# 80 tokens' experts gathered instead of 64, with the one-hots and the gates' copies dealt out anew

## The chip, the core and the metric

The kernel runs on one core of a Trainium2 chip. Its engines work side by side: TensorE (PE; its weight loads are the row PEld), VectorE (DVE), ScalarE (ACT), GpSimd (POOL) and SyncE (SP), the last of which here only issues transfers. They meet by semaphores. Matrix products go into PSUM banks, everything else lies in SBUF (128 partitions). The metric is the device time of one execution, in microseconds.

## The reference

One layer of an encoder step for 288 tokens (256 of a prompt, 32 new ones), each a row of 2048 numbers in fp32: differential attention, attention into 256 memory rows, an output projection, a norm, then a mixer of experts, and a second norm. The change is about the mixer. It has 128 x 128 experts, each one row of `u_tab` and one of `v_tab`. A token picks 16 of them in each of 8 heads, so 128 in all, by the sums of two scores (first key, second key):

```python
q = (xt @ w_q).reshape(T, 8, 2, 128)
s = jnp.einsum('thcd,hcnd->thcn', q, sub_keys)
sv, si = lax.top_k(s, 16)
cand = (sv[:, :, 0, :, None] + sv[:, :, 1, None, :]).reshape(T, 8, 256)
cidx = (si[:, :, 0, :, None] * 128 + si[:, :, 1, None, :]).reshape(T, 8, 256)
best, pos = lax.top_k(cand, 16)
experts = jnp.take_along_axis(cidx, pos, axis=-1).reshape(T, 128)
gates = jax.nn.softmax(best, axis=-1).reshape(T, 128)
...
    act = jnp.einsum('td,tkd->tk', xs, u_tab[es])
    h = jax.nn.gelu(act, approximate=False) * gs
    return jnp.einsum('tk,tkd->td', h, v_tab[es])
```

The result is `layer_norm(ALPHA * x1 + peer_ffn(x1))` with `x1` the rows behind the first norm.

## The kernel before

**Two ways for the mixer.** For 224 tokens (`ND`, the dense ones) every expert is computed, and the gates, mostly zero, pick. For the last 64 tokens the rows of their own experts are gathered from DRAM.

**The stream.** Everything large (projection weights, 256 units of `u_tab`, 256 of `v_tab`; a unit is 128 x 1024 numbers, 512 KB) is in a list `plan`, in the order of its use. `stream` (L131) keeps it running ahead of TensorE: SyncE loads a unit into one of four `raw` tiles, ScalarE casts it to the upper part `hi` (L165), VectorE makes `lo = raw - hi` (L181), both in three tiles in turn, up to two units ahead. So each product of fp32 numbers is made as two or three products of parts.

**Activations of the dense tokens** (from L1025). `x1` of the dense tokens lies in `ux` as [hi | lo], 2 x 224 columns. A block of 128 experts has two units of 8 pairs: L1039 multiplies `hi` weights with all 448 columns, L1041 `lo` weights with 224. `finish_act` adds the two halves of the bank (ScalarE's copy L992, an identity product L994) and applies GELU into `bigA` (the first 96 blocks, `SPLIT`) or `bigB`.

**Gates of the dense tokens.** From block 64 (`G0`) on, each unit also advances `gate_jobs`. For two tokens `one_hots` makes the one-hots of the second key on VectorE (L970) and those of the first key, with the gate as their height, on ScalarE (four instructions, L974 and L975); L1019 multiplies them, so that a bank gets the 128 x 128 gates of four tokens. `gate_in` brings these to the blocks: where the activation is already there VectorE multiplies it (L985), where it isn't VectorE copies the gates aside (L987), and `finish_act` multiplies later (L1004). With two tokens a unit this takes 112 units.

**The gathered tokens.** Their choices are made first: `topk` works on two heads at once, four heads of 64 tokens on each half of the partitions, so that a partition stands for a token and one of two groups of heads. `Rows` then fetches half rows of 1024 numbers by indirect DMA on GpSimd's queue (L948) into a ring of three tiles: when VectorE has used a half row, the third after it is issued. There are 64 steps of two half rows, 128 for `u_tab` (`use_u`, L963, a product with `x1g` and its sum) and 128 for `v_tab` (`use_v`, L1111, a multiple of the row added to `vacc`). They are spread evenly over the units: the first 40 (`GFIRST`) ahead of block 64, the rest up to the end of the activations; those of the values up to unit 230 (`VEND`).

**Values** (from L1199). Two halves of the columns, 128 units each; L1200 multiplies `hi` values with [hi | lo] of the gated activations (448 columns), L1202 `lo` values with 224, into eight banks that stay for a half. The last two or three units of a half form a group in which one bank after the other ends: `evac` copies (L1117), adds by a product (L1119) and sums into `yT` (VectorE, L1120); in the second half `turn` (L1190) transposes `yT` into banks that are free, and VectorE takes statistics (L1193) for the second norm of the dense tokens behind it.

**Work beside the stream.** A `tick`, two to a unit in the activations and one to a unit in the values, lets each generator in `stages` take a step, and the first one in `slow` spend its `pace`, by the cost that each step yields. So `topk`, `rows_job` (the rows `x1g`) and, behind the last gathered value, `finish_gathered` are paid out. `finish_gathered` folds the upper half of the partitions onto the lower (a transfer, then L1146), normalises the 64 rows (statistics L1151; ScalarE L1159; L1161 and L1163) and stores them (L1164). What of `slow` is left when the last group of values begins is issued at once, between that group's splits and its products.

## Time and profile before

| | us |
|---|---|
| median of three runs | 2014.75 |
| lowest, highest | 2012.73, 2016.01 |
| span of the profiled execution, first to last instruction | 2008.1 |
| median less span (the profiled execution is not timed apart) | 6.7 |
| activations with gates, 960 to 1290 us: PE, DVE, ACT busy, of 330.0 | 330.0, 302.7, 310.3 |
| values, 1360 to 1900 us: PE, DVE, ACT busy, of 540.0 | 539.7, 455.9, 271.4 |
| transfers in these two stretches | 297 and 327 GB/s |

The busy time of an engine in a stretch says how near it is to setting the pace there; the share over the whole span mixes stages. TensorE overlaps its instructions, so that their durations add to more than the time: the distance from one start to the next is what one costs.

### The profile page before, as it was taken

The numbers are of one execution on the slowest core, as the hardware profiler recorded it, in microseconds if no ns is written. First come the engines' busy times: TensorE is split into PE (matmuls) and PEld (weight loads), VectorE is DVE, ScalarE is ACT, GpSimd is POOL, SyncE is SP. The second block draws the span as 40 slices with busy tenths as digits, with TensorE's granted clock in tenths as the row PEclk, the third lists the DMA queues.
The fourth block names the chain that finished last, engine by engine and source line by source line (L and its number), as shares of the span: only waits on it lengthen the run. The fifth ranks groups of instructions, "written<-read, shape, count | busy, mean of one in ns | idle before, by whom it ended". The sixth has DMA issues, their size and how long they took to land.

```text
span 2008.1 us, 34989 instructions
## 1 busy us (share of the span) xinstructions
PE 1983.6 (99%) x13178; PEld 1872.5 (93%) x13178; DVE 1567.3 (78%) x2683; ACT 1160.7 (58%) x1919; POOL 480.9 (24%) x348
## 2 busy tenths in 40 slices
PE   9999999999999999999999999999999999999996
PEld 7999999999999999999999999999999999999996
DVE  5455555556788889998899999978888888888886
ACT  5345545544534555555999999854455555444553
POOL 0110000010000112222333333324443343334412
PEclk9999999999999999999999999999999999999998
DMA  8854555484445788888888888889999998999985
GB/s 294 258 165 141 153 155 153 129 287 137 154 148 162 241 291 280 277 282 283 294 298 296 293 298 302 300 288 318 335 322 343 327 333 314 323 328 321 327 264 167
DMA packets 147625, 521.21 MB, mean 260 GB/s; under 512 B 16848, under 2 KB 21088, under 8 KB 147328
## 3 DMA queue, kind: packets, MB, share of 16 engines
q1 hardware_dynamic: 103504, 360.49, 54.8%
q0 software_dynamic: 43952, 158.48, 22.0%
q8 instruction: 104, 1.70, 0.3%
q14 instruction: 65, 0.53, 0.1%
HBM read 508.33 MB, written 10.06 MB: 258 GB/s over the span
## 4 chain that ended last, share of the span: by engine, by line
PE 96%; DMA 1%; DVE 1%; ACT 1%; POOL 0%; issue 0%; SPq 0%; POOLq 0%; ACTq 0%; DVEq 0%
PE pa L1039 22%; PE pa L1200 11%; PE pb L1200 11%; PE pa L1041 11%; PE pa L232 8%; PE pa L233 7%; PE pa L234 7%; PE pb L1202 5%; PE pa L1202 5%; PE pb L1019 3%; DMA raw<-in_wmk 1%; PE pa L994 1%; PE pb L397 0%; DVE lo L181 0%; PE pa L893 0%; PE pa L319 0%
## 5 line engine op out<-in xcount | busy, mean ns | idle before, releaser
L181 DVE TENSOR_TENSOR lo<-raw,hi 128x1024 fp32r<-128x1024 f32 (+1 forms) x679 | 820.8, 1211 | 367.1 <-ACT hi L165 356.7
L165 ACT CAST hi<-raw 128x1024 fp32r<-128x1024 f32 (+1 forms) x679 | 705.5, 1040 | 497.2 <-PE pa L1200 253.8
L1039 PE MATMUL pa<-ux,hi 128*128 128x448 f32 x2048 | 669.8, 379 | 0.0
L1041 PE MATMUL pa<-ux,lo 128*128 128x224 f32 x2048 | 543.6, 265 | 0.0
L1039 PEld LDWEIGHTS pa<-ux,hi 128*128 128x128 f32 x2048 | 385.4, 188 | 29.4 <-issue 0.2
L1041 PEld LDWEIGHTS pa<-ux,lo 128*128 128x128 f32 x2048 | 391.7, 191 | 0.0
L948 POOL DMA_INDIRECT ur<-in_u,gidx x128 | 197.9, 1546 | 700.2 <-DVE ur L963 329.8
L1200 PE MATMUL pa<-hs,hi 128*128 128x448 f32 x1020 | 338.3, 376 | 0.0
L1200 PE MATMUL pb<-hs,hi 128*128 128x448 f32 x1020 | 338.0, 376 | 0.0
L948 POOL DMA_INDIRECT vr<-in_v,gidx x128 | 221.4, 1730 | 354.7 <-DVE x1g L1111 321.2
L1202 PE MATMUL pb<-hs,lo 128*128 128x224 f32 x1020 | 271.1, 266 | 0.3 <-DVE lo L181 0.3
L1202 PE MATMUL pa<-hs,lo 128*128 128x224 f32 x1020 | 271.0, 266 | 0.0
L1200 PEld LDWEIGHTS pb<-hs,hi 128*128 128x128 f32 x1020 | 191.4, 188 | 17.5
L1200 PEld LDWEIGHTS pa<-hs,hi 128*128 128x128 f32 x1020 | 191.4, 188 | 17.4
L1202 PEld LDWEIGHTS pb<-hs,lo 128*128 128x128 f32 x1020 | 195.1, 191 | 0.5 <-DVE lo L181 0.5
L232 PE MATMUL pa<-xh,hi 128*128 128x288 f32 x640 | 195.2, 305 | 0.0
L1202 PEld LDWEIGHTS pa<-hs,lo 128*128 128x128 f32 x1020 | 195.1, 191 | 0.0
L233 PE MATMUL pa<-xl,hi 128*128 128x288 f32 x640 | 188.9, 295 | 0.0
L234 PE MATMUL pa<-xh,lo 128*128 128x288 f32 x640 | 188.2, 294 | 0.0
L1111 DVE SCALAR_TENSOR_TENSOR x1g<-vr,ggate,x1g 128x1024 f32<-128x1024 f32 x128 | 163.7, 1279 | 0.0
L963 DVE SCALAR_TENSOR_TENSOR ur<-ur,x1g 128x1024 f32<-128x1024 f32 x128 | 155.7, 1216 | 0.0
L232 PEld LDWEIGHTS pa<-xh,hi 128*128 128x128 f32 x640 | 120.0, 188 | 4.9 <-issue 3.7
(346 smaller groups left out, 2706.7 us busy)
## 6 DMA issues: line engine op xcount, KB each, us to landing
raw<-in_ut SPq DMA_DIRECT2D x256, 512.0 KB, 4.4
raw<-in_v SPq DMA_DIRECT2D x255, 512.0 KB, 6.5
raw<-in_win SPq DMA_DIRECT2D x80, 512.0 KB, 3.7
raw<-in_wq SPq DMA_DIRECT2D x32, 512.0 KB, 3.6
raw<-in_wo SPq DMA_DIRECT2D x29, 512.0 KB, 3.7
raw<-in_wmv SPq DMA_DIRECT2D x8, 512.0 KB, 5.3
raw<-in_wmk SPq DMA_DIRECT2D x6, 512.0 KB, 5.8
xn<-in_xn POOLq DMA_DIRECT2D x8, 384.0 KB, 9.7
```

The costliest lines, as they stand in the source:

```text
L165: nc.scalar.copy(hi[:, cs], raw[:, cs])
L181: nc.vector.tensor_sub(lo, raw, hi.bitcast(F32))
L232: nc.tensor.matmul(ps[:, :n], wh, mh[:, d, :n], start=(d == 0), stop=False)
L233: nc.tensor.matmul(ps[:, :n], wh, ml[:, d, :n], start=False, stop=False)
L234: nc.tensor.matmul(ps[:, :n], wl, mh[:, d, :n], start=False, stop=(d == DT - 1))
L948: nc.gpsimd.indirect_dma_start(out=t, out_offset=None, in_=self.table, in_offset=bass.IndirectOffsetOnAxis(ap=gidx[:, a, s:s + 1], axis=0))
L963: nc.vector.scalar_tensor_tensor(rows, rows, 1.0, x1g[:, a * 1024:(a + 1) * 1024], op0=OP.mult, op1=OP.mult, accum_out=gact[:, a, s:s + 1])
L1039: nc.tensor.matmul(ps[:, :2 * ND], wh, ux[:, d].rearrange("p a t -> p (a t)"), start=(d == 0), stop=False, skip_group_check=True)
L1041: nc.tensor.matmul(ps[:, :ND], wl, ux[:, d, 0], start=False, stop=False, skip_group_check=True)
L1111: nc.vector.scalar_tensor_tensor(va, rows, ggate[:, s:s + 1], va, op0=OP.mult, op1=OP.add)
L1200: nc.tensor.matmul(accs[dt][:, :2 * ND], wh, hb.rearrange("p a t -> p (a t)"), start=(i == 0), stop=False, skip_group_check=True)
L1202: nc.tensor.matmul(accs[dt][:, :ND], wl, hb[:, 0], start=False, stop=False, skip_group_check=True)
```

## The change

16 tokens more, numbers 208 to 223, have their experts gathered. They get 32 steps' halves of their own: their 8 heads lie on 8 groups of 16 partitions in a second tile `x1b`, which is filled by eight small transfers, and steps from 64 on use it. So `ND` is 208, the dense products have 416 and 208 columns, the gates take 104 units, and there are 160 half rows for each table. `gathered_choice` waits for a ninth selection of the gathered tokens (`topk([(2, 4, 20)])`, one head for 128 partitions). `topk` does two heads in one instruction where it can. The one-hots of the second key are made for four tokens at once; `gate_in`'s copies go to ScalarE. `finish_gathered` folds `vacc` once and `x1b` three times (64, 32, 16 rows), moves 16 rows behind the 64, and has the norm on 80. `SPLIT` becomes 88 and the buffers of `xr` five. Cut to its core:

```diff
-ND = 224
+ND = 208
+NA = 224
+SLOTS = 80
+STEPS = 2 * SLOTS
-SPLIT = 96
+SPLIT = 88
-GFIRST = 40
+GFIRST = 48
...
+        for h in range(8):
+            nc.gpsimd.dma_start(x1b[16 * h:16 * h + 16], xn[80:96, 1])
+        for x, own_rows in ((x1g, xn[:, 2]), (x1b, x1b)):
...
+            nc.gpsimd.dma_start(s_all[16 * h:16 * h + 16, 20], s_all[80:96, 8 + h])
...
-                        slow.insert(at1 + 1, gathered_choice())
+                        slow.insert(at1 + 1, topk([(2, 4, 20)]))
+                        slow.insert(at1 + 2, gathered_choice())
...
     def use_u(s, a, rows):
+        x = x1g if s < 64 else x1b
...
+    def second_hots(t0):
+        Bt = big[2].tile([P, 4, NKEY], F32, tag="ohB", name=f"ohB{t0}")
+        nc.vector.tensor_tensor(out=Bt, in0=iota.unsqueeze(1).to_broadcast([P, 4, NKEY]),
+                                in1=e2T[:, t0:t0 + 4].unsqueeze(2).to_broadcast([P, 4, NKEY]), op=OP.is_equal)
+        return Bt
...
             if a < n:
-                nc.vector.tensor_copy(bt[:, a:n, t0:t0 + 4], pg[:, i0 + a:i0 + n])
+                nc.scalar.copy(bt[:, a:n, t0:t0 + 4], pg[:, i0 + a:i0 + n])
...
-                    ug.upto(GFIRST + (128 - GFIRST) * (n + 1 - 2 * G0) // (2 * (NKEY - G0) - 4))
+                    ug.upto(GFIRST + (STEPS - GFIRST) * (n + 1 - 2 * G0) // (2 * (NKEY - G0) - 4))
...
-        up = [gat.tile([P, 1024], F32, tag="rows", name=f"up{c}") for c in range(2)]
-        for c in range(2):
-            nc.gpsimd.dma_start(up[c][:64], vacc[64:128, c * 1024:(c + 1) * 1024])
-        yield 4.0
...
+        for x, w in ((vacc, 64), (x1b, 64), (x1b, 32), (x1b, 16)):
+            up = [gat.tile([P, 1024], F32, tag="rows", name=f"up{num()}") for c in range(2)]
+            for c in range(2):
+                nc.gpsimd.dma_start(up[c][:w], x[w:2 * w, c * 1024:(c + 1) * 1024])
+            yield 4.0
+            for c in range(2):
+                cs = slice(c * 1024, (c + 1) * 1024)
+                nc.vector.tensor_add(x[0:w, cs], x[0:w, cs], up[c][:w])
+                yield 1.15
+        nc.gpsimd.dma_start(vacc[64:SLOTS], x1b[0:16])
         yield 4.0
...
-                vg.upto(128 * (n + 1 - v_from) // (VEND - v_from))
-                if vg.used == 128:
+                vg.upto(STEPS * (n + 1 - v_from) // (VEND - v_from))
+                if vg.used == STEPS:
                     slow.append(finish_gathered())
```

The first place is VectorE among the units with gates. Before, two units and a bit of them (lines as above: splits L181, one-hots L970, gates L985 and L987, a gathered half row L963, the late product L1004):

```order
L181 TENSOR_TENSOR lo_12842<-raw_12767,hi_12841 128x1024
L970 TENSOR_TENSOR ohB_12864<-iota,e2T 128x256
L985 TENSOR_TENSOR bigA<-bigA,pb_12794 128x92x4
L987 COPY bigA<-pb_12794 128x4x4
L987 COPY bigB<-pb_12794 128x32x4
L963 SCALAR_TENSOR_TENSOR ur_0_12721,gact<-ur_0_12721,x1g 128x1024
L181 TENSOR_TENSOR lo_12884<-raw_12806,hi_12883 128x1024
L970 TENSOR_TENSOR ohB_12909<-iota,e2T 128x256
```

VectorE after the change, at a like place; the lines are 1 to 13 numbers later there (L184 are the splits, L964 the half rows, L990 the gates, L1009 the late product):

```order
L184 TENSOR_TENSOR lo_11570<-raw_11494,hi_11569 128x1024
L970 TENSOR_TENSOR ohB_11595<-iota,e2T 128x512
L964 SCALAR_TENSOR_TENSOR ur_1_11486,gact<-ur_1_11486,x1g 128x1024
L1009 TENSOR_TENSOR bigA<-bigA,tmp_11592 128x52
L184 TENSOR_TENSOR lo_11608<-raw_11532,hi_11607 128x1024
L990 TENSOR_TENSOR bigA<-bigA,pb_11557 128x78x4
L964 SCALAR_TENSOR_TENSOR ur_0_11527,gact<-ur_0_11527,x1g 128x1024
L184 TENSOR_TENSOR lo_11648<-raw_11572,hi_11647 128x1024
```

The copies L987 are gone from VectorE, a one-hot instruction stands in every second unit, and half rows stand in more of the units.

ScalarE in the same stage, before (casts L165, one-hots L974 and L975, `finish_act` L992, L1000 and L1002):

```order
L974 ACTIVATE ohA_13803<-iota,e1T 128x128
L975 ACTIVATE ohA_13803<-ohA_13803,gT,ngT 128x128
L992 CAST small_13818<-pa_13740 128x224
L165 CAST hi_13821<-raw_13744 128x1024
L1000 ACTIVATE tmp_13844<-pa_13740 128x160
L1002 ACTIVATE bigB<-pa_13740 128x64
```

ScalarE after (casts L168, one-hots L979 and L980, the gates' copies L992, `finish_act` L997, L1005 and L1007):

```order
L979 ACTIVATE ohA_11552<-iota,e1T 128x128
L980 ACTIVATE ohA_11552<-ohA_11552,gT,ngT 128x128
L992 COPY bigA<-pb_11479 128x11x4
L992 COPY bigB<-pb_11479 128x40x4
L997 CAST small_11566<-pa_11490 128x208
L168 CAST hi_11569<-raw_11494 128x1024
L1005 ACTIVATE tmp_11592<-pa_11490 128x52
L1007 ACTIVATE bigA<-pa_11490 128x156
```

The two copies of a bank's gates now stand on ScalarE ahead of the small copy and the next cast.

The second place is VectorE at the end of the values, in the last group (L1120 are the sums into `yT`, L1193 the statistics of transposed rows). Before:

```order
L181 TENSOR_TENSOR lo_21682<-raw_21629,hi_21681 128x1024
L181 TENSOR_TENSOR lo_21702<-raw_21653,hi_21701 128x256 x4
L1120 SCALAR_TENSOR_TENSOR yT<-yT,pb_18636 128x224
L1120 SCALAR_TENSOR_TENSOR yT<-yT,pb_18639 128x224
L1120 SCALAR_TENSOR_TENSOR yT<-yT,pb_18644 128x224
L1193 BN_STATS nst_15445<-pb_21753 128x6
```

VectorE there after (L1159 is a fold's addition, L1167 to L1143 the statistics and what follows from them, L1177 and L1179 the norm's rows, L1133 the sums into `yT`):

```order
L184 TENSOR_TENSOR lo_21532<-raw_21488,hi_21531 128x256 x4
L1159 TENSOR_TENSOR x1b<-x1b,up_21412 16x1024
L1167 BN_STATS nst_21545<-x1g 80x6 x4
L1141 BN_AGGR nmr_21546<-nst_21545 80x2
...
L1143 SCALAR_TENSOR_TENSOR nmr_21546<-nmr_21546 80x1
L1177 TENSOR_TENSOR x1g<-x1g,gb_21543 80x1024
L1179 TENSOR_TENSOR x1g<-x1g,gb_21544 80x1024
L1177 TENSOR_TENSOR x1g<-x1g,gb_21568 80x1024
L1179 TENSOR_TENSOR x1g<-x1g,gb_21569 80x1024
L1133 SCALAR_TENSOR_TENSOR yT<-yT,pb_18445 128x208
L1133 SCALAR_TENSOR_TENSOR yT<-yT,pb_18448 128x208
```

The last fold and the whole norm of the gathered tokens, which before stand among earlier units, now stand between the last split and the first sum into `yT`.

GpSimd's queue at the same place after (L1161 moves the 16 rows, L1146 are norm rows, L1180 and L1181 stores):

```order
L1161 DMA x1g<-x1b 16x2048
L1146 DMA gb_21543<-in_lnrow 80x1024
L1146 DMA gb_21544<-in_lnrow 80x1024
L1180 DMA out_y<-x1g 64x1024
L1181 DMA out_y<-x1g 16x1024
L1146 DMA gb_21568<-in_lnrow 80x1024
L1146 DMA gb_21569<-in_lnrow 80x1024
```

Here the second pair of norm rows stands behind the stores of the first half; it goes into tiles of the ring of three.

## Rows read from the trace of the kernel before

**Rows 1.** The page, parts 1 and 2: engines, and GB/s in 40 slices.
```profile
PE 1983.6 (99%) x13178; PEld 1872.5 (93%) x13178; DVE 1567.3 (78%) x2683; ACT 1160.7 (58%) x1919; POOL 480.9 (24%) x348
...
GB/s 294 258 165 141 153 155 153 129 287 137 154 148 162 241 291 280 277 282 283 294 298 296 293 298 302 300 288 318 335 322 343 327 333 314 323 328 321 327 264 167
```

**Rows 2.** Groups by line: count, then busy us, mean ns, and idle time before.
```profile
L1039 PE MATMUL pa<-ux,hi 128*128 128x448 f32 x2048 | 669.8, 379 | 0.0
L1200 PE MATMUL pa<-hs,hi 128*128 128x448 f32 x1020 | 338.3, 376 | 0.0
```

**Rows 3.** Timeline of TensorE in the activations: start and duration in us.
```profile
702.89 0.38 PE L1039 MATMUL pa<-ux,hi 128*128 128x448 f32 x1
703.11 0.27 PE L1041 MATMUL pa<-ux,lo 128*128 128x224 f32 x1
703.22 0.27 PE L994 MATMUL pa<-small,identr 128*128 128x224 f32 x1
703.32 0.38 PE L1039 MATMUL pa<-ux,hi 128*128 128x448 f32 x1
```

**Rows 4.** Timeline of TensorE's weight loads at the same place.
```profile
703.11 0.19 PEld L994 LDWEIGHTS pa<-small,identr 128*128 128x128 f32 x1
703.22 0.19 PEld L1039 LDWEIGHTS pa<-ux,hi 128*128 128x128 f32 x1
```

**Rows 5.** Timeline of TensorE in the memory's and the first projections.
```profile
60.30 0.40 PE L319 MATMUL pa<-lo,memh 128*128 128x512 f32 x1
60.53 0.40 PE L320 MATMUL pa<-hi,meml 128*128 128x512 f32 x1
...
90.12 0.29 PE L234 MATMUL pa<-xh,lo 128*128 128x288 f32 x1
90.25 0.30 PE L232 MATMUL pa<-xh,hi 128*128 128x288 f32 x1
```

**Rows 6.** Stretches: us; busy PE, PEld, DVE, ACT, POOL; clock; DMA share; GB/s.
```profile
420.00:422.00 2.00, 2.00 (x17) 2.00 (x16) 1.93 (x9) 0.65 (x1) 0.58 (x1) 1.00 1.02 397
960.00:1290.00 330.00, 330.00 (x2235) 315.67 (x2234) 302.65 (x587) 310.25 (x708) 121.42 (x77) 1.00 0.85 297
1360.00:1900.00 540.00, 539.73 (x3409) 509.89 (x3409) 455.90 (x395) 271.40 (x275) 217.44 (x129) 1.00 0.93 327
```

**Rows 7.** ScalarE's groups by line and shape, 960 to 1290 us; L616: whole run.
```profile
L165 ACT CAST hi<-raw 128x1024 fp32r<-128x1024 f32 x109 | 113.8, 1044 | 0.0
...
L616 ACT COPY ot<-pa 128x128 f32<-128x128 f32 x16 | 4.3, 272 | 0.0
```

**Rows 8.** Groups by line and shape, VectorE, 1360 to 1900 us.
```profile
L181 DVE TENSOR_TENSOR lo<-raw,hi 128x1024 fp32r<-128x1024 f32 x213 | 260.7, 1225 | 82.3 <-ACT hi L165 75.4
L1111 DVE SCALAR_TENSOR_TENSOR x1g<-vr,ggate,x1g 128x1024 f32<-128x1024 f32 x121 | 154.8, 1279 | 0.0
```

**Rows 9.** Gathers: issues 1350 to 1930 us (median to landing); line 948, both tables.
```profile
vr<-in_v,gidx POOLq DMA_INDIRECT x125, 8.2
...
DMA to landing us min/median/max: 4.0/7.3/11.1
```

**Rows 10.** The end: timelines of VectorE and TensorE; VectorE's groups 1925 to 1975; issues.
```profile
1981.87 0.39 DVE L1120 SCALAR_TENSOR_TENSOR yT<-yT,pb 128x224 f32<-128x224 f32 x1 [0.88 <-PE pb L1119]
...
1983.79 0.60 PE L1190 MATMUL pb<-ident,yT 128*128 128x128 f32 x4
...
L1151 DVE BATCH_NORM_STATS2 nst<-x1g 64x6 f32<-64x512 f32 x4 | 2.6, 675 | 0.0
L1161 DVE TENSOR_TENSOR x1g<-x1g,gb 64x1024 f32<-64x1024 f32 x2 | 2.4, 1208 | 0.0
L261 DVE RECIPROCAL rs<-rs 64x1 f32<-64x1 f32 x1 | 0.2, 156 | 1.4 <-ACT rs L259 1.4
...
out_y<-x1g POOLq DMA_DIRECT2D x2, 256.0 KB, 4.4
```

**Rows 11.** Timeline of VectorE in the query projection; in brackets the idle time before.
```profile
535.89 1.23 DVE L181 TENSOR_TENSOR lo<-raw,hi 128x1024 fp32r<-128x1024 f32 x1 [3.40 <-ACT hi L165]
```

More of the change, by code (lines that the diff above doesn't have):

```diff
@@ L679, in topk @@
[L679 to L685 removed]
+        n, t, R = len(units), units[0][0], ROWS[units[0][0]]
+        key = f"{t}_{units[0][1]}"
+        step = units[-1][1] - units[0][1] or 1
+        hs = slice(units[0][1], units[-1][1] + 1, step)
@@ new lines, in new @@
+        def new(tag, shape, dt=F32):
+            return tw.tile([P, 2] + shape, dt, tag=tag, name=f"{tag}{key}")[:R, :n]
+        S = [s_all[:R, u] for *_, u in units]
+        sv, si, sf = new("sv", [2, K]), new("si", [2, K], U32), new("sf", [2, K])
+        s2, ca, pos = new("s2", [2, NKEY]), new("ca", [K, K]), new("pos", [K], U32)
+        ab, abf = new("ab", [2, K], U32), new("abf", [2, K])
+        bv = best[:R, t, hs]
+        both = [(q, c) for c in range(2) for q in range(n)]
+        for q, c in both:
+            V.max(out=sv[:, q, c, 0:8], in_=S[q][:, c])
@@ L742, in gates @@
+        yield 0.62 * n
+        for c, en in ((0, e1n), (1, e2n)):
+            V.tensor_reduce(out=en[:R, t, hs], in_=eq[c], op=OP.add, axis=AX.X)
+        yield 0.62 * n
     def gates(t, nh):
@@ L1006, in gate_jobs @@
     def gate_jobs():
-        hots, banks = {}, {}
+        first, second, banks = {}, {}, {}
         n2 = ND // 2
@@ L1073, in tile_stream_step @@
         stages.append(g)
-    assert ug.used == 128 and gated == ND
+    assert ug.used == STEPS and gated == ND
     ohs.close()
```

202 lines of the change are left out of this document (89 added, 113 removed).

## The prediction

> **What bounds the kernel now.** I read the page first: TensorE is busy in 99% of the span, and no other engine comes near that [rows 1]. Then the groups of instructions by line and shape: the two expert stages hold 2048 pairs of products in the activations (lines 1039 and 1041) and 2 x 1020 in the values (lines 1200 and 1202, in two kinds of banks), 4088 in all [rows 2]. Then TensorE's timeline, since the durations of the groups overlap and only the distance between two starts says what an instruction costs: the product with 448 columns holds the engine 0.22 us, the one with 224 columns 0.10 to 0.11 [rows 3]. In neither stage does TensorE stand idle, so the span is the sum of these distances. The other engines are read by stage: while the gates are made (960 to 1290 us) ScalarE is busy 310 of 330 us and VectorE 303; in the values (1360 to 1900 us) VectorE is busy 456 of 540 us and the transfers run at 327 GB/s with the DMA engines 93% busy [rows 6]. So TensorE is the bound, with three followers close behind it.
>
> **What a pair loses.** The change takes 16 tokens out of the dense products: 448 columns become 416, 224 become 208. Beyond that the count of products stays. Longer products give the slope: 512 columns are 0.23 us apart, 288 columns 0.13 [rows 5], so (0.23 - 0.13) / 224 = 0.45 ns a column, and the long product loses 32 x 0.45 = 14.3 ns. The short one is another matter. Weights of 128 columns are loaded before each product, and two loads follow each other 0.11 us apart at the closest [rows 4]; where two short products stand in a row (line 994 behind line 1041) they too take 0.11 and 0.10 us [rows 3]. The load has the same size whatever the number of tokens, so I take the short product to be at the load's pace already and to lose nothing. Ends: 0 for the pair if both halves are held by loads, 14.3 + 16 x 0.45 = 21.5 ns if none is. I take 14.3, since [rows 3] and [rows 4] show the same 0.11. Sum: 4088 x 14.3 ns = 58.5 us. The Trainium skill ("TensorE: Matmul & The Clock Gate", Back-to-back issue gap) gives an isolated product N/2.4 + 2.5 ns; by that, an estimate, a pair would go from 285 to 265 ns and the change would bring 82 us. The trace has 0.32 us a pair, so the rule misses what the loads cost, and the sum goes by the rows.
>
> Fewer tokens also have gates. A unit (half an expert, 8 pairs) takes 330 / 109 = 3.03 us with gates [rows 6, 7] and 8 x 0.317 + 0.05 = 2.58 without; 208 tokens need 104 such units, not 112, so 8 x 0.45 = 3.5 us go. **TensorE's part: 62 us.** A unit then wants 8 x 14.3 = 115 ns less: 2.92 us with gates, 2.42 in the values.
>
> **What the followers give back, stage by stage.** With gates: ScalarE is busy 310.25 / 109 = 2.85 us a unit now [rows 6, 7]. It gets 75 copies that VectorE made before (87 there), 104 columns on average; a copy of 128 columns from PSUM takes it 0.27 us [rows 7]. That is 75 x 0.27 / 104 = 0.19 us a unit at most, and some 0.11 if neighbours overlap by 0.1 us. ScalarE would want 2.95 to 3.03 us where TensorE wants 2.92. VectorE stays where it is: 2.78 us a unit now, plus (112 - 88)/124 = 0.19 more half rows (by the code's spread over 124 units) at 1.3 us = +0.24, less 0.07 for four one-hots in one instruction, less 0.15 for the copies: 2.80. I take 2.95 us a unit, as casts run ahead of TensorE by up to two units and cover a little: 104 x 0.035 = **3.6 us back**; ends 0 (all covered) and 104 x 0.115 = 12 (no gain here).
>
> Values: the pace is 540 / 213 = 2.535 us a unit [rows 8]. 160 half rows instead of 128 come between units 8 and 230, 0.72 a unit instead of 0.57. VectorE: 456/213 = 2.14 us, plus 0.15 x 1.28 [rows 8] = 2.33 of 2.42, still enough. Transfers: (1 + 0.72) x 0.524 MB and a few small ones = 0.914 MB in 2.42 us = 378 GB/s, where the stage moves 327 now and the whole trace holds 397 at a share of 1.02 for a while [rows 6]. Gathers: three tiles are in turn, each issued when the third before it is used, so a half row has 3 x 2.535 / 0.57 = 13.4 us less 1.6 for its own use and issue to land; it needs 8.2 [rows 9]. Afterwards it has 3 x 2.42 / 0.72 - 1.6 = 8.5. Both limits end within a few per cent of TensorE's pace. I take 2.45 us for the 222 units with gathers: **7 us back**; ends 0 and 140 (if every landing took the 11.1 us of the slowest [rows 9]: 0.24 x 12.7 = 3.05 us a unit).
>
> The end: the routine that closes the gathered tokens is paid out by its cost, one unit's worth a tick. It had some 22 to spend in 26 units; now four folds instead of one bring some 45, and the order shows what is left over to be drained between VectorE's last split and its first product sum of the last group, and ScalarE's part ahead of its first small copy there. In order, from the end of the last split: add 1.2; a transfer of 128 KB 4.4 (the output's 4.4, for 256 KB); four statistics 2.6; the rest of the norm 2.6, of which 1.4 wait for ScalarE; ScalarE's scaling 1.2, taken as VectorE's for such a tile; multiply and add 2.4; then GpSimd issues two stores before the next norm rows, 1.1, and these land in 4.4; two more operations 2.4: 22.3 us [rows 10]. Today the first product sum starts 0.9 us after the last split (0.88, to 1981.87), and TensorE's first transposes at 1983.79 [rows 10]. These need a bank of the four that hold the sums, free only when VectorE has read it: TensorE stands for about **20 us**, which nothing hides. Ends 14 (transfers at 2.5 us) and 26 (at 7, or TensorE's clock down after the pause).
>
> At nothing I cost the early part: eight small transfers and four operations of 1.2 us for the second x1 tile, and a ninth selection, go where VectorE waits up to 3.4 us for casts [rows 11]; about 3 us if that cover were gone.
>
> **Sum.** 62 - 3.6 - 7 - 20 = 31.4 us. The profiled execution spans 2008.1 us; the median of the runs, 2014.75, is 6.7 above it, for what lies around the span. 2008.1 - 31.4 + 6.7 = 1983 us. 0.2%, 4 us, is about what a measurement of this kernel can tell from no change.
>
> **Rivals.**
> 1. The ring of gathers becomes the bound of the values (slower). A unit then takes 0.24 x (landing + 1.6) us. For it: the margin shrinks from 3.6 us to 0.3, and more load lengthens landings. Against: the slowest landing now, 11.1 us [rows 9], is still inside its 11.8, and a full ring slows itself. Midway between the median and the slowest, 9.65 us: 2.70 us a unit, 222 x 0.25 = 56 us more, 2039. From a landing of 9.2 us it is slower than before.
> 2. The transfers have a ceiling below 378 GB/s. The best slice of the values is 343 [rows 1]; with that as ceiling a unit takes 0.914 / 0.343 = 2.665, 48 us more: 2031. The stretch at 397 speaks against it. The Trainium skill ("DMA: Bandwidth & Descriptors", Specifications) lists about 358 GB/s of HBM for a core; by that, an estimate, 2.55 us a unit and 2006. The same 397 is above the rule.
> 3. The gates' stretch gains nothing, ScalarE being full: 12 instead of 3.6 back, 1991.
> 4. Less is lost: short products shrink too (152 units without gates x 8 x 7.2 ns = 9 us: 1974), or the drained end is short (1963 if it costs nothing).
> 5. The pairs don't shorten at all: 58.5 us missing, while the followers' 10.6 fall away; the end remains: 2014.75 - 3.5 + 20 = 2031.
>
> **How the numbers follow.** Forecast 0.48, its own range 1968 to 2000 with the bounds above; rival 1: 0.10; rival 2: 0.12, half of it below 2010; rival 3: 0.10; rival 4: 0.17; rival 5: 0.03. Faster: 0.48 + 0.10 + 0.17 and some 0.03 of rival 2 = 0.78; slower 0.10 + 0.05 + 0.03 = 0.18; within 0.2%: 0.04. The range 1955 to 2028 leaves out rival 1, the worse part of 2, rival 5 and the outermost of 4.
>
> **What would show it.** Starts of the long product 0.20 us apart and of the short one still 0.10 to 0.11: the pair; if 0.096, rival 4. Gate units at 2.92 to 2.97 us with ScalarE at 99%; at 3.03, rival 3. Values at 2.42 to 2.47 us with gathers landing in under 8.7 us; VectorE's long waits on a gathered tile would be rival 1, casts waiting for raw rows, with the DMA share at 1, rival 2. At the end a stretch of some 15 to 20 us in which TensorE waits for VectorE. If TensorE waits in mid-stage for a split, the sum is wrong there.

## The result, and the profile after

The changed kernel takes **2032.24 us** (median of four runs, 2031.67 to 2035.03) where the kernel before takes 2013.95 in the same comparison. It is slower by a ratio of 1.0099, 95% interval 1.0085 to 1.0113 (such ratios are estimated from the single executions; the quotient of the two medians is 1.0091). Forecast was 1983, faster than before, with a range of 1955 to 2028. The profiled execution of the changed kernel took 2035.03 us, its span 2033.3. One execution of an experiment, 2268.16 us at a granted clock of 0.753 in the kernel with its end paid faster, is left out of what follows.

The page of the changed kernel, parts 1 and 2 (compare [rows 1]):

```profile
PE 1953.6 (96%) x13146; PEld 1874.5 (92%) x13146; DVE 1618.0 (80%) x2569; ACT 1154.3 (57%) x1962; POOL 609.6 (30%) x437
...
PEclk9999999999999999999999999999999999999996
...
GB/s 290 265 167 137 156 147 157 149 267 127 177 139 180 247 320 297 303 301 320 326 318 320 317 314 315 339 291 369 351 362 347 359 347 343 361 376 362 352 230 117
```

TensorE is busy 30 us less, and the span is 25 us longer. Where it stands is seen by cutting both spans at the starts of units (the first product of a unit on TensorE's timeline; a unit is 8 pairs). In us, with the same cuts for the experiments below:

| profiled execution | to unit 0 | act. 0-127 | act. 128-231 | act. 232-255 | val. 0-125 | 126-129 | 130-229 | 230-251 | last group, end | span |
|---|---|---|---|---|---|---|---|---|---|---|
| before | 624.6 | 330.7 | 314.6 | 66.0 | 319.6 | 11.8 | 253.3 | 55.7 | 31.6 | 2008.1 |
| **after** | 626.0 | 323.2 | 327.2 | 66.0 | 321.0 | 12.9 | 247.7 | 54.8 | 54.4 | 2033.3 |
| copies on VectorE | 628.3 | 320.9 | 305.1 | 65.6 | 319.2 | 13.6 | 247.0 | 55.5 | 54.3 | 2009.5 |
| end paid faster | 629.8 | 320.2 | 327.1 | 65.7 | 320.2 | 12.7 | 250.4 | 64.1 | 39.8 | 2029.9 |
| ring of four | 625.3 | 320.1 | 329.1 | 65.0 | 310.2 | 12.8 | 243.3 | 56.7 | 54.1 | 2016.6 |
| half the stream's bytes | 628.0 | 320.7 | 328.3 | 66.2 | 303.7 | 11.5 | 240.7 | 52.9 | 54.0 | 2005.9 |
| three together | 632.1 | 320.3 | 305.7 | 65.4 | 328.9 | 11.5 | 250.4 | 56.1 | 32.9 | 2003.3 |
| early folds | 630.0 | 321.2 | 326.2 | 66.5 | 345.2 | 12.6 | 262.3 | 58.3 | 32.8 | 2055.1 |
| copies first | 630.1 | 320.9 | 307.1 | 65.8 | 314.7 | 13.1 | 248.5 | 55.4 | 52.9 | 2008.3 |
| no more half rows | 629.0 | 319.8 | 323.6 | 60.5 | 303.7 | 12.7 | 240.7 | 52.9 | 53.0 | 1996.0 |
| three, by SyncE | 627.4 | 321.0 | 305.5 | 65.9 | 322.4 | 13.4 | 244.5 | 56.6 | 31.0 | 1987.8 |
| early folds, by SyncE | 630.1 | 320.3 | 327.1 | 64.8 | 344.7 | 11.5 | 256.9 | 54.6 | 32.3 | 2042.3 |
| before, copies on ScalarE | 627.5 | 330.7 | 336.4 | 68.7 | 319.6 | 12.2 | 253.3 | 56.1 | 31.5 | 2036.2 |
| three, accumulating | 629.2 | 322.1 | 303.7 | 65.0 | 315.0 | 15.1 | 245.0 | 55.2 | 32.4 | 1982.6 |

Each row is one execution. Beside the experiments the kernel before took 2013.08 to 2013.96 us (medians), so that their times can be compared. The executions of the kernels with folds in the middle of the values (early folds, three together, by SyncE, accumulating) scatter by 13 to 26 us, and the rows of early folds, three together and early folds by SyncE show one from the upper end; differences of a few us between these rows say little.

Units 128 to 231 are those with gates after the change (before they go on to 239). So the change loses 12.6 us in the gates, gains only 4 in all the values up to the last group, and loses 22.8 at the end.

**The pairs are shorter, as forecast.** TensorE's timeline in the values of the changed kernel (start, duration; compare [rows 3]):

```profile
1399.75 0.37 PE L1217 MATMUL pb<-hs,hi 128*128 128x416 f32 x1
1399.96 0.26 PE L1219 MATMUL pb<-hs,lo 128*128 128x208 f32 x1
1400.06 0.36 PE L1217 MATMUL pb<-hs,hi 128*128 128x416 f32 x1
1400.27 0.26 PE L1219 MATMUL pb<-hs,lo 128*128 128x208 f32 x1
1400.36 0.37 PE L1217 MATMUL pb<-hs,hi 128*128 128x416 f32 x1
```

Three starts of the long product are 0.31 and 0.30 us apart, 0.32 before. Over all pairs of the values the median distance from the long product to the short one is 204 ns, and from the short one to the next long one 96, where they were 214 and 103. The median unit, which is an undisturbed one, takes 2.409 us (2.533 before).

**But units are disturbed.** Stretches of the changed kernel (us; busy PE, PEld, DVE, ACT, POOL; clock; DMA share; GB/s; compare [rows 6]):

```profile
960.00:1250.00 290.00, 279.76 (x1887) 266.79 (x1886) 259.92 (x418) 271.14 (x667) 116.10 (x83) 1.00 0.91 319
1360.00:1900.00 540.00, 525.92 (x3427) 512.03 (x3426) 483.60 (x427) 267.25 (x274) 273.06 (x159) 1.00 0.97 356
```

TensorE, idle 0.3 us at most in these stages before, stands 10 and 14 us in them. Its weight loads (PEld) wait longer than that, since a product already begun keeps TensorE busy for part of such a wait.

### The profile page after: what moved, and what is told of

The parts are those of the page before. It is cut to its first block, busy times and chain, and to the rows that moved or that the text cites. A ratio compares the mean times of both kernels' runs of the same rounds, so it can differ in the third digit from the quotient of the medians.

```text
span 2033.3 us, 35148 instructions
## 1 busy us (share of the span) xinstructions
PE 1953.6 (96%) x13146; PEld 1874.5 (92%) x13146; DVE 1618.0 (80%) x2569; ACT 1154.3 (57%) x1962; POOL 609.6 (30%) x437
## 4 chain that ended last, share of the span: by engine, by line
PE 54%; DMA 19%; DVE 13%; issue 7%; ACT 3%; POOL 3%; DVEq 0%; SPq 0%; POOLq 0%; ACTq 0%
PE pa L1048 11%; DMA raw<-in_v 10%; PE pa L235 8%; PE pa L236 7%; PE pa L237 7%; DMA vr<-in_v,gidx 6%; DVE lo L184 6%; PE pa L1050 5%; PE pa L1217 2%; POOL ur L948 2%; PE pb L1217 2%; DVE x1g L1124 2%; DVE ur L964 1%; ACT hi L168 1%; DMA ur<-in_u,gidx 1%
## 5 line engine op out<-in xcount | busy, mean ns | idle before, releaser
L184 DVE TENSOR_TENSOR lo<-raw,hi 128x1024 fp32r<-128x1024 f32 (+1 forms) x679 | 816.3, 1207 | 283.0 <-ACT hi L168 276.5
L168 ACT CAST hi<-raw 128x1024 fp32r<-128x1024 f32 (+1 forms) x679 | 706.5, 1041 | 509.6 <-DMA raw<-in_v 228.0
L1048 PE MATMUL pa<-ux,hi 128*128 128x416 f32 x2048 | 644.0, 373 | 0.0
L1050 PE MATMUL pa<-ux,lo 128*128 128x208 f32 x2048 | 532.3, 260 | 6.6 <-DVE lo L184 6.5
L948 POOL DMA_INDIRECT ur<-in_u,gidx x160 | 252.1, 1576 | 451.0 <-DVE ur L964 251.7
L948 POOL DMA_INDIRECT vr<-in_v,gidx x160 | 283.5, 1772 | 298.1 <-DVE x1g L1124 242.2
L1217 PE MATMUL pb<-hs,hi 128*128 128x416 f32 x1020 | 328.2, 368 | 0.0
L1217 PE MATMUL pa<-hs,hi 128*128 128x416 f32 x1020 | 324.6, 368 | 0.0
L1219 PE MATMUL pb<-hs,lo 128*128 128x208 f32 x1020 | 269.7, 264 | 15.2 <-DVE lo L184 14.7
L1219 PE MATMUL pa<-hs,lo 128*128 128x208 f32 x1020 | 264.4, 259 | 0.0
L964 DVE SCALAR_TENSOR_TENSOR ur<-ur,x1g 128x1024 f32<-128x1024 f32 x128 | 155.6, 1216 | 5.8 <-DMA ur<-in_u,gidx 5.8
```

Of the source, the lines that this page charges most:

```text
L168: nc.scalar.copy(hi[:, cs], raw[:, cs])
L184: nc.vector.tensor_sub(lo, raw, hi.bitcast(F32))
L948: nc.gpsimd.indirect_dma_start(out=t, out_offset=None, in_=self.table, in_offset=bass.IndirectOffsetOnAxis(ap=gidx[:, a, s:s + 1], axis=0))
L964: nc.vector.scalar_tensor_tensor(rows, rows, 1.0, x[:, a * 1024:(a + 1) * 1024], op0=OP.mult, op1=OP.mult, accum_out=gact[:, a, s:s + 1])
L1048: nc.tensor.matmul(ps[:, :2 * ND], wh, ux[:, d].rearrange("p a t -> p (a t)"), start=(d == 0), stop=False, skip_group_check=True)
L1050: nc.tensor.matmul(ps[:, :ND], wl, ux[:, d, 0], start=False, stop=False, skip_group_check=True)
```

## The gates: a wait, not a full engine

Waits of the changed kernel, 960 to 1250 us (engine, its instruction, what it waited for: us in all, times, longest):

```profile
PEld pa L999 <- ACT small L997: 21.9, 46, 1.9
PE pa L999 <- ACT small L997: 9.0, 32, 1.6
ACT bigB L992 <- DVE bigB L990: 8.1, 22, 0.5
ACT bigA L992 <- DVE bigA L990: 3.6, 12, 1.6
```

TensorE's loads wait 21.9 us for ScalarE's small copies, a wait that before has no line at all in this stage. The 9.0 us of its products lie inside these: together they cover 22.0 us, not the 31 that the text on record below adds up. That is about what the next two experiments give back. ScalarE in turn waits 11.7 us for VectorE's products of the gates. One case, on ScalarE's timeline (in brackets the idle time before):

```profile
1099.78 0.16 ACT L992 COPY bigA<-pb 128x4 f32<-128x4 f32 x1 [0.23 <-DVE bigA L990]
1099.84 0.30 ACT L992 COPY bigB<-pb 128x160 f32<-128x160 f32 x1
1100.02 0.35 ACT L997 CAST small<-pa 128x208 fp32r<-128x208 f32 x1
```

and on TensorE's, load and product:

```profile
1100.43 0.19 PEld L999 LDWEIGHTS pa<-small,identr 128*128 128x128 f32 x1 [0.46 <-ACT small L997]
1100.43 0.36 PE L999 MATMUL pa<-small,identr 128*128 128x208 f32 x1 [0.20 <-ACT small L997]
```

The copies stand behind VectorE's product out of the same bank (L990), the small copy stands behind the copies, the identity product behind the small copy, and everything else of TensorE behind that. Theory A: the wait costs the time. Theory B: ScalarE, with a busy time of 2.94 us a unit (282.43 us in the 302 of units 128 to 223), has too much to do. A third, that the additional half rows keep VectorE too busy, is rival B of the first experiment.

**Copies on VectorE.** One line goes back:

```diff
-                nc.scalar.copy(bt[:, a:n, t0:t0 + 4], pg[:, i0 + a:i0 + n])
+                nc.vector.tensor_copy(bt[:, a:n, t0:t0 + 4], pg[:, i0 + a:i0 + n])
```

> The changed kernel, only with the early gates' copies given back to VectorE. In the changed kernel a unit with gates takes 3.14 us where 2.95 was forecast, and TensorE waits 31 us for ScalarE's small copies there. Theory A (ScalarE stands behind VectorE: its copies of a bank wait for VectorE's product of the same bank, 12 us of recorded waits, and so come late for the small copy): a unit falls to 2.95 to 2.98 us, 104 x 0.17 = 18 us, the time is about 2014. Rival B (more half rows keep VectorE too busy, whoever copies): VectorE has 0.15 us more per unit, the time stays or rises by up to 10, 2030 to 2042.

Measured: 2012.98 us, 0.9994 of the kernel before (0.9978 to 1.0010). The 104 units take 305.1 us, 2.93 each: 22 less than after, and 9.5 less than the same units before. That is the gain that the change has in this stage if its copies stay where they were, and the half rows, which are as many as after, do not prevent it.

**Copies first.** The same work on the same engines, in the other order:

```diff
+            if a < n:
+                nc.scalar.copy(bt[:, a:n, t0:t0 + 4], pg[:, i0 + a:i0 + n])
+        for i0, n, bt in big[:2]:
+            a = min(max(done - i0, 0), n)
             if a > 0:
...
-            if a < n:
-                nc.scalar.copy(bt[:, a:n, t0:t0 + 4], pg[:, i0 + a:i0 + n])
```

> The changed kernel, only that a bank's early gates are copied by ScalarE ahead of VectorE's products of the same bank, so that ScalarE doesn't wait for these; the work of both engines is the same. Theory A (the wait behind VectorE, 12 us of the stage, makes the small copies late): 104 units go from 3.14 to about 3.0 us, 12 to 15 less, 2018. Theory B (ScalarE has simply too much: 282 us of busy time in 96 units, 2.94 a unit, where TensorE would take 2.93): a unit stays at 3.08 or more, 2026 or above.

Measured: 2013.86 us, 1.0008 (0.9995 to 1.0021); the 104 units take 307.1 us, 2.95 each. Its stretch and two of its waits:

```profile
951.00:1258.00 307.00, 307.00 (x2129) 301.41 (x2128) 292.02 (x468) 299.87 (x746) 162.22 (x93) 1.00 0.94 337
```

```profile
DVE bigA L994 <- ACT bigB L989: 9.4, 25, 0.7
...
PEld pa L1001 <- ACT small L999: 2.4, 14, 0.2
```

ScalarE is busy 98% and TensorE never idle: now VectorE waits for ScalarE, 9.4 us, and that hurts nobody. The row also shows what ties the two together: VectorE's product into `bigA` waits for the copy into `bigB`, another tile. What they share is the bank that both read, though other columns of it. Theory B falls: the same ScalarE work costs 2 us against the copies on VectorE (307.1 and 305.1 us) if the copies don't wait, and 22 if they do (327.2), so the wait itself costs 20.

**Before, with the copies on ScalarE.** The one part alone, on the kernel before (`nc.vector.tensor_copy` to `nc.scalar.copy` in `gate_in`):

> The kernel before (224 dense tokens, 64 gathered), only with the early gates' copies moved to ScalarE, behind VectorE's products of the same bank. By the wait found in the changed kernel (undoing it or turning the order round brought 20 to 22 us of 104 units): the 112 units with gates go from 3.03 to about 3.15 us or more, 13 to 20 us slower, 2027 to 2034. If the move only hurts at the shorter pace of 208 tokens: 2010 to 2016.

Measured: 2037.84 us, 1.0118 (1.0099 to 1.0136); the units 128 to 231 take 21.8 us more than before. Two of its waits, 960 to 1290 us:

```profile
PEld pa L994 <- ACT small L992: 22.3, 49, 0.5
...
ACT bigA L987 <- DVE bigA L985: 11.6, 31, 0.4
```

So this part of the change loses by itself, at 224 dense tokens too, and more than the whole change does (24.8 us by the medians, against 18.3).

## The values: landings that come just too late

Waits of the changed kernel, 1360 to 1900 us:

```profile
ACT hi L168 <- DMA raw<-in_v: 207.7, 151, 3.4
...
DVE x1g L1124 <- DMA vr<-in_v,gidx: 30.2, 38, 2.1
...
PEld pb L1219 <- DVE lo L184: 24.5, 42, 1.3
```

VectorE waits 30 us for gathered half rows (before it waited for none), the splits behind these waits come late, and TensorE's loads wait 24.5 us for the splits. ScalarE now waits for the stream's loads 151 times, 207.7 us (before 22 times, 32.1 us). The transfers run at 356 GB/s, 97% busy. Theory A: the ring of three is too short for its landings. Theory B: the transfers are at a ceiling. Theory C: VectorE is full.

**Ring of four.** A fourth tile for the values' half rows, in what the gates' one-hots leave free:

```diff
-                t = gat.tile([P, 1024], F32, tag="rows", name=f"{self.name}{s}_{a}")
+                pool = more if self.depth == 4 and g % 4 == 3 else gat
+                t = pool.tile([P, 1024], F32, tag="rows", name=f"{self.name}{s}_{a}")
...
-                self.fetch(g + 3)
+                self.fetch(g + self.depth)
...
+    more = ctx.enter_context(tc.tile_pool(name="more", bufs=1, side="right"))
...
-    vg = Rows(v_rows, "vr", use_v)
+    vg = Rows(v_rows, "vr", use_v, 4)
```

> The changed kernel, only that the gathered rows of the values have four tiles in turn instead of three. The values up to the last group take 607.6 us for 240 units, 2.53 a unit, with undisturbed units at 2.41. Theory A (the ring is too short for a landing of 8.3 us): half rows come 3.3 us earlier relative to their use, VectorE's 34 us of waits for them go and the units come to 2.41 to 2.44; 22 to 29 us less, 2003 to 2010. Rival B (the transfers are at their ceiling, 353 GB/s): a longer ring only lets more wait in the queue; landings grow to about 11 us, the units stay within 0.02 us, 2027 to 2036.

Measured: 2019.79 us, 1.0031 (1.0015 to 1.0047), 12 less than after. Its issues and its stretch, 1360 to 1900 us:

```profile
vr<-in_v,gidx POOLq DMA_INDIRECT x156, 8.4
```

```profile
1360.00:1900.00 540.00, 534.44 (x3524) 526.98 (x3524) 496.90 (x440) 275.18 (x282) 288.79 (x164) 1.00 0.98 367
```

Landings stay at 8.4 us (8.3 after), the transfers do 367 GB/s, and the units 0 to 125 and 130 to 229 come to 2.46 and 2.43 us, from 2.55 and 2.48. So 356 was no ceiling, and the ring held the units. But 9 of the 24 us above 2.41 a unit remain, and TensorE's loads still wait 9.2 us for splits.

**Half the stream's bytes.** In the values the first 512 columns of each unit but the last are loaded, and cast twice (the other columns' values are left out):

```diff
+            if k in VHALF:
+                two = raw[:, :512].unsqueeze(1).to_broadcast([P, 2, 512])
+                h2, l2 = (w.rearrange("p (a b) -> p a b", a=2) for w in (hi, lo))
+                nc.scalar.copy(h2, two)
+                pending.append((k, h2, l2, two))
...
-            for cs in pieces(k):
+            for cs in [slice(0, 512)] if k in VHALF else pieces(k):
                 nc.sync.dma_start(raw[:, cs], src[:, cs])
```

> The changed kernel, only that of each unit of the values the first 512 of 1024 columns are loaded and cast twice: ScalarE, VectorE and TensorE have the same work, the stream's transfers in the values have half the bytes, the gathers all of theirs (the values' other columns are left out of the sums). Theory B (the transfers' ceiling): demand falls from 0.914 to 0.652 MB a unit, 270 GB/s at 2.41 us, the units come to 2.41 to 2.43, 26 us less, about 2006. Theory A (the ring): only as much as landings shorten with the load; if they stay above 8 us, the waits for gathered rows stay, and the time is above 2020. Theory C (VectorE is full, 2.3 of 2.41 us): nothing changes, 2030.

Measured: 2008.21 us, 0.9968 (0.9954 to 0.9982), 24 less than after; the units take 2.41 us throughout. Its issues and stretch, 1360 to 1900 us:

```profile
vr<-in_v,gidx POOLq DMA_INDIRECT x157, 6.4
```

```profile
1360.00:1900.00 540.00, 539.58 (x3587) 536.50 (x3587) 510.30 (x448) 282.09 (x288) 276.18 (x167) 1.00 0.80 266
```

With 266 GB/s moved, landings take 6.4 us and a ring of three is enough. VectorE does more in the same time here (510.3 us) than after: theory C falls. A and B don't exclude each other: the load lengthens the landings, and the ring gives them no room. The Trainium skill ("DMA: Bandwidth & Descriptors", Specifications) lists about 358 GB/s of HBM for a core. The changed kernel's 356 agrees with it; the 367 with a ring of four, over 540 us, is above it, so the measurement decides that it did not set the pace here.

**No more half rows.** The experts of the 16 tokens are left out, the dense products stay at 208 (`STEPS = 128`, `gact` set to zero):

> The changed kernel, with 128 half rows of each table as before: the 16 tokens are taken out of the dense products, and their experts are left out. It shows what the shorter products bring where the gathers don't grow. By the undisturbed distances of the changed kernel's trace (0.300 us a pair, 0.317 before) the values come to 2.41 us a unit, 3 to 5 us for all above 240 x 2.41 = 578 where the changed kernel has 607.6: 25 less, and some 5 us less in the activations without gates: about 2002. If it is not the gathers that disturb the values but the stream at the faster pace, the values stay above 2.47 us a unit: 2016 or more.

Measured: 2001.29 us, 0.9949 (0.9930 to 0.9968). The values come to 303.7 and 240.7 us, the same as with half the stream's bytes; the last 24 units of the activations to 60.5 us, from 66.0. So the 16 tokens' half rows themselves cost the 24 us of the values and 5.5 us there; without them a unit of the values takes 2.41 us, where 2.42 was forecast for TensorE alone. In the gates they cost little: these still take 323.6 us, 3.6 less than after. Since this kernel still has the gates' wait and the long end, it is not the change's best. What holds the last units of the activations is in the waits of the changed kernel, 1277 to 1342 us (before, VectorE has no such line; without the additional half rows it is 0.2 us):

```profile
DVE ur L964 <- DMA ur<-in_u,gidx: 7.9, 10, 3.1
...
PEld pa L1050 <- DVE lo L184: 3.4, 4, 2.2
```

## The end: drained, and hard to place

VectorE's timeline at the end of the changed kernel (compare [rows 10]):

```profile
1981.81 1.43 DVE L184 TENSOR_TENSOR lo<-raw,hi 128x256 fp32r<-128x256 f32 x4 [0.54 <-ACT hi L168]
1983.16 1.21 DVE L1159 TENSOR_TENSOR x1b<-x1b,up 16x1024 f32<-16x1024 f32 x1
1987.52 2.47 DVE L1167 BATCH_NORM_STATS2 nst<-x1g 80x6 f32<-80x512 f32 x4 [3.15 <-DMA x1g<-x1b]
...
1993.10 1.22 DVE L1177 TENSOR_TENSOR x1g<-x1g,gb 80x1024 f32<-80x1024 f32 x1 [1.36 <-ACT x1g L1175]
...
2002.41 1.22 DVE L1177 TENSOR_TENSOR x1g<-x1g,gb 80x1024 f32<-80x1024 f32 x1 [6.83 <-DMA gb<-in_lnrow]
...
2004.81 0.92 DVE L1133 SCALAR_TENSOR_TENSOR yT<-yT,pb 128x208 f32<-128x208 f32 x3
```

ScalarE's (the routine's scaling L1175, the copy L1130) and TensorE's, there:

```profile
1991.83 2.37 ACT L1175 ACTIVATE x1g<-x1g,nmr 80x1024 f32<-80x1024 f32 x2 [1.22 <-DVE nmr L1143]
1994.11 0.54 ACT L1130 CAST vsm<-pb 128x208 fp32r<-128x208 f32 x2
...
1994.47 0.54 PE L1132 MATMUL pb<-vsm,identr 128*128 128x208 f32 x1 [10.63 <-ACT vsm L1130]
1994.81 0.59 PE L1217 MATMUL pb<-hs,hi 128*128 128x416 f32 x1
...
1995.37 0.59 PE L1217 MATMUL pb<-hs,hi 128*128 128x416 f32 x1
...
2005.23 1.12 PE L1207 MATMUL pb<-ident,yT 128*128 128x128 f32 x4 [6.44 <-DVE yT L1133]
```

Between VectorE's last split (over at 1983.24) and its first sum (2004.81) lie 21.6 us of the routine, as forecast (22.3). TensorE stands 10.6 us for ScalarE's copy, which is behind the routine's scaling, and 6.4 us for VectorE; between the two, long products start 0.56 us apart, not 0.30: after the pause TensorE runs at the lower of its two levels, as its granted clock shows (the column behind the busy times, 0.50):

```profile
1994.80:1998.50 3.70, 3.70 (x15) 3.60 (x14) 0.78 (x1) 0.33 (x1) 2.11 (x4) 0.50 0.36 80
```

**End paid faster.** One line, where the routine is appended:

```diff
                     slow.append(finish_gathered())
+                    pace["rate"] = 2.2
```

> The changed kernel, only that the routine which closes the gathered tokens is paid out 2.2 units of cost a tick instead of 1.0 once it is appended, so that nothing of it is left to be issued at once in the last group. Theory A (the drained rest makes TensorE stand 10.6 and 6.4 us and run at the lower clock behind it): the last group and the tail come back to those of before, 21 us less, about 2011. Rival B (VectorE then waits for the folds' transfers among the splits, and the loss only moves there): at most 8 us less, 2024 to 2032.

Measured: 2030.25 us (median of four executions, 2024.91 to 2031.66), 1.0067 (1.0046 to 1.0088), little better than after. The end comes to 39.8 us, but units 230 to 251 go from 54.8 to 64.1: the end shrinks as in theory A, and most of the loss only moves, as in rival B. VectorE waits for the routine's transfers in the middle of splits, as in this row of its timeline:

```profile
1982.96 1.22 DVE L1177 TENSOR_TENSOR x1g<-x1g,gb 80x1024 f32<-80x1024 f32 x1 [5.32 <-DMA gb<-in_lnrow]
```

**Early folds.** The 16 tokens' steps come first in the values, and their three folds are paid out in the middle, in pieces of 512 columns with 8 units between a transfer and its addition; the end has one fold, as before:

```diff
+    def fold_late():
+        for w in (64, 32, 16):
+            for c in range(4):
+                cs = slice(c * 512, (c + 1) * 512)
+                up = upp.tile([P, 512], F32, tag="up", name=f"up{num()}")
+                nc.gpsimd.dma_start(up[:w], x1b[w:2 * w, cs])
+                yield 8.0
+                nc.vector.tensor_add(x1b[0:w, cs], x1b[0:w, cs], up[:w])
+                yield 0.6
...
+    vg = Rows(v_rows, "vr", use_v, first=64)
```

> The changed kernel, only with the 16 tokens' steps first in the values and their folds paid out in the middle. Paying the whole routine faster moved the loss (the stretch from unit 230 to 252 went from 54.8 to 64.1 us, the end from 54.4 to 39.8). Theory A (it is the amount of work and waits behind the last gathered row that costs, wherever it stands): the end comes to 32 to 36 us with 54 to 56 before it, 18 to 22 less, 2010 to 2014. Rival B (the end is slow for another reason, such as the last pieces' loads or the clock): the end stays above 45 us, 2023 or more.

Measured: 2046.41 us, 1.0136 (1.0105 to 1.0167). The end is at 32.8 us, so what was drained there is what it cost, 22 us. But the values take 24 and 15 us more, with seven units of 4.9 to 11.8 us (the text on record below has 6.7 as the lower end): a loss that neither theory had.

**Three together** (copies on VectorE, ring of four, early folds):

> The changed kernel with three things together: the early gates' copies on VectorE, four tiles in turn for the gathered rows of the values, and the 16 tokens' steps taken first in the values, their three folds paid out in small pieces over some 100 units in the middle, so that the end has one fold as in the kernel before. If the three losses are separate, the sum is 2032 less 19 (copies, measured), less 12 (ring, measured), less 20 (end): 1981, 1.6% below the kernel before. If the losses stand for each other (a stage sped up only waits longer for transfers, which are at 367 of some 370 GB/s in the values with the longer ring), about 1995. If the early folds cost VectorE as much in the middle as they save at the end: 2000.

Measured: 1997.97 us, 0.9911 (0.9887 to 0.9934). It beats both kernels, but is 17 us above the plain sum (1981); three units of the values take 9.5 to 11 us. Gathers are late there because GpSimd's gather instruction itself takes up to 12 us. The first suspect is GpSimd's queue, which also issues the folds' transfers and the residual's loads.

**Three together, small transfers by SyncE** (`nc.gpsimd.dma_start` to `nc.sync.dma_start` for `up` and for `yT`), and **early folds by SyncE** (for `up` alone):

> The kernel with the three things together, only that the small transfers which it and the kernels before have on GpSimd's queue in the values (the folds of the 16 tokens, and the eight loads of the residual) are issued by SyncE. In the kernel with the three things GpSimd's gather instruction takes 11 to 12 us in three places instead of 1.7, each behind such transfers, and three units of the values take 9.5 to 11 us. Theory A (the small transfers hold up GpSimd's queue and with it the gathers): these go, 3 x 8 us and some more, about 1972. Rival B (the gathers are held up by their own number, with four tiles in turn): the long instructions stay, 1990 to 2000.

> The kernel with the early folds alone, only that the folds' transfers are issued by SyncE, not GpSimd. With them on GpSimd the end came to 32.8 us as forecast, but the values before it took 42 us more than in the changed kernel, with seven units of 6.7 to 11.8 us. Theory A (queue): the values come back to about 321 + 13 + 248, the end stays at 33: 2010. Rival B (the additions in the middle cost VectorE what they cost): the values stay 15 us or more above, 2027 or more.

Measured: 1998.11 us, 0.9936 (0.9913 to 0.9960), and 2040.38 us, 1.0117 (1.0092 to 1.0141). No gain; the long instructions stay. The queue theory falls. GpSimd's timeline of the early folds by SyncE shows a usual one and a long one (the rows' unit is us again):

```profile
1505.25 1.68 POOL L951 DMA_INDIRECT vr<-in_v,gidx  x1 [1.11 <-DVE x1g L1128]
...
1509.79 9.04 POOL L951 DMA_INDIRECT vr<-in_v,gidx  x1 [2.08 <-DVE x1g L1128]
1519.13 0.94 POOL L951 DMA_INDIRECT vr<-in_v,gidx  x1 [0.30 <-issue]
```

and VectorE's beside it:

```profile
1509.43 0.68 DVE L1161 TENSOR_TENSOR x1b<-x1b,up 64x512 f32<-64x512 f32 x1
1510.04 1.21 DVE L184 TENSOR_TENSOR lo<-raw,hi 128x1024 fp32r<-128x1024 f32 x1
...
1515.63 2.34 DVE L184 TENSOR_TENSOR lo<-raw,hi 128x1024 fp32r<-128x1024 f32 x2
1526.26 1.28 DVE L1128 SCALAR_TENSOR_TENSOR x1g<-vr,ggate,x1g 128x1024 f32<-128x1024 f32 x1 [8.28 <-DMA vr<-in_v,gidx]
```

The gather instruction starts 0.36 us into a fold's addition and ends at 1518.83, 0.86 us after VectorE has run out of work at 1517.97. In the values of the four kernels with such additions 25 gather instructions take over 4 us, and 20 of them start 0.35 us after an addition's start (the text on record below says 13 where 14 are meant). The 0.35 us by itself says little: most gather instructions start so long after the start of whatever VectorE runs. The share says more: of the 32 that start within an addition 20 take over 4 us, of the 529 that start within a split 5 do, and of the 66 that start while VectorE is idle none takes over 0.97. So the next suspect is VectorE.

**Three together, accumulating.** The folds are transfers that add in place, so VectorE has no addition for them (against three together, cut):

```diff
-                nc.gpsimd.dma_start(up[:w], x1b[w:2 * w, cs])
-                yield 8.0
-                nc.vector.tensor_add(x1b[0:w, cs], x1b[0:w, cs], up[:w])
-                yield 0.6
+            nc.gpsimd.dma_start(x1b[0:w], x1b[w:2 * w], accum_op=OP.add)
+            yield 12.0
```

> The kernel with the three things together, only that the three folds of the 16 tokens in the middle of the values are accumulating transfers on GpSimd's queue (32 to 64 rows added in place), so that VectorE has no addition for them. Moving the folds' plain transfers to SyncE left long gather instructions (7 to 11 us on GpSimd, where 1.7 is usual) in place; 5 of the 6 over 4 us, and 11 of 13 in the other two such kernels, start 0.35 us behind the start of a fold's addition on VectorE, and end only when VectorE stands idle. Theory A (VectorE's additions, put between its other work, keep GpSimd from its instruction): without them none is above 4 us, the values come to those of the kernel with the longer ring alone (310 + 13 + 243 us), the end stays at 32 to 33, and the span is about 1974, the time 1977. Rival B (any further transfer in the middle upsets the ring, or VectorE is too full with any order): long gather instructions stay, the time stays at 1990 to 2000.

Measured: **1984.38 us**, 0.9856 (0.9832 to 0.9880). No gather instruction of the values takes over 4 us, the end is at 32.4 us, the units with gates at 2.92 us. Against the ring of four alone the values still take 5 and 2 us more, and the time is 7 above theory A's 1977. The edit also makes three transfers of twelve; that this, and not the missing additions, ended the long instructions was not tried apart, but the shares above speak for the additions. Its issues in the values, with the first of the three accumulating transfers:

```profile
vr<-in_v,gidx POOLq DMA_INDIRECT x150, 8.4
...
x1b<-x1b POOLq DMA_DIRECT2D x1, 512.0 KB, 12.3
```

It beats the kernel before by 1.4%, the changed kernel by 48 us.

## Why the prediction was wrong, step by step

- **The pair**: right in size, wrong in its parts. Forecast 14.3 ns less for a pair, all of it from the long product; an undisturbed unit of 8 pairs lost 124 ns, 15.5 a pair; by the median distances, which add to a little more, 10 from the long product and 7 from the short one. The step "the short product is at the load's pace already" failed: it went to 96 ns, below the 0.11 us of [rows 4], which was thus no bound. This is the sign that the prediction gave for rival 4. That the size is right all the same is partly luck: the long product lost 4 ns less than forecast, the short one 7 more.
- **The gates**: this step failed by far, and is the largest of the misses. Forecast 3.6 us back, with ends 0 and 12. Measured, the 104 units took 327.2 us where the sum has 104 x 2.95 = 307, and where the same units took 305 and 307 us once the copies did not wait: 20 to 22 more. The sum counted ScalarE's busy time and asked whether it fits; it does (98% in the kernel with the copies first). What it did not ask, though the order of instructions showed the copies ahead of the small copy, is what the copies themselves wait for: VectorE's product out of the same bank. Rival 3 named the place, with the wrong reason and half the price.
- **The values**: the mechanism was right, the term mis-sized. Forecast 2.45 us a unit and 7 us back; measured 2.55 and 2.48, and 24 us above undisturbed units. The margin of 0.3 us between 8.5 to be had and 8.2 needed was read as enough; with landings that scatter up to 11 us [rows 9] it was none. Landings did not grow much (8.3 us), so the price was less than half of rival 1's 56 us. Rival 2 gave 2.665 us by a ceiling of 343 GB/s. By the Trainium skill's 358 ("DMA: Bandwidth & Descriptors", Specifications) it would be 2.55, an estimate. The first half of the values came to that, though not for that reason, as the ring of four shows.
- **The last units of the activations** (232 to 255): forecast 6 us less, none measured. The sum put the gathers' limits only on the values; here VectorE waits for gathered rows as well, and without the additional rows the 24 units take 60.5 us.
- **The end**: right. Forecast 20 us, measured 22.8, by the parts that were named; TensorE's lower clock behind the pause, which stood at the upper end, did come.
- **The early part at nothing**: right ahead of the first unit, 1.4 us. But units 0 to 127 were 7.5 us shorter instead of 14.7: the sum put no follower on them. From 626 to 949 us TensorE's loads wait 5.8 us for VectorE's splits, where before they wait for none. Some 3 of these lie in one unit (5.39 us, from 697.8 us on), ahead of which VectorE waits 3.8 us for the first gathered half row. In the experiments with 208 dense tokens these units took 320 to 322 us, so 9 to 11 of the 14.7 come; VectorE is busy 234 of 249 us there (700 to 949 us), and what keeps the rest was not tried.

Added up, in us by which the stages are longer than in the sum: 0 to 127 7 us, gates 21, the last activations 6, the values 18, the end 3, ahead of them 1: the 56 us between 2008.1 - 31.4 and 2033.3. That the best of the experiments comes to 1984, next to the forecast of 1983, is chance: the forecast has 20 us for the end in it, which that kernel does not pay, so by the forecast's own terms it should have come to 1963.

## What to carry to other kernels

Before an instruction is moved to an engine with room, read in the order what it will wait for there and who stands behind it in that engine's queue: the engine's busy time says nothing about that, and the other order of the same two instructions was worth 18 us here. A margin of a few per cent between the median landing time and the time that a ring allows was a loss already, since landings scatter; count the ring's tiles again whenever the pace or the number of gathers changes. A routine that is paid out by its cost must be counted against the ticks that are left, and where it is moved to, its effect on the queues there has to be looked at anew.

## What was not expected of the hardware

GpSimd's gather instruction takes 0.94 us where VectorE is idle and mostly 1.68 where it isn't. Beside dense VectorE work it took 2.6 to 3.75 us now and then in the values of the changed kernel and up to 5.75 us in its activations (before, 2.07 at most), and up to 12.3 us in the kernels with folds on VectorE. All thirteen instructions of 9 us and more in the values of these four kernels ended 0.8 to 0.9 us after VectorE had run out of work; the shorter ones over 4 us mostly ended without such a gap. The Trainium skill ("SBUF — State Buffer", Who interferes with whom) says that the two engines share a pair of ports, that a VectorE instruction with two inputs in SBUF contends with a GpSimd instruction that reads SBUF, and, of VectorE's two-port modes, that whoever issues first has the pair for the whole instruction. The traces agree that the gather takes longer beside such instructions (every VectorE row of the early folds by SyncE above has two inputs in SBUF, and the gather reads its row numbers there). But the 9.04 us span eight VectorE instructions, not one: the wait did not end with the instruction that it met. No run here shows the ports themselves. Why an addition of 0.68 us sets it off, and a split of 1.2 us mostly not, stays open.
